# w_conv_out in two seven-product units behind three gate pairs, in the mixer of a two-layer encoder trunk

## The chip, the core and the metric

The kernel runs on one core of a Trainium2 chip. The metric is the device time of one launch in microseconds. Engines are named as the profile names them: PE (TensorE's matmuls), PEld (its weight loads), DVE (VectorE), ACT (ScalarE), POOL (GpSimd), SP (SyncE, which issues the weight loads here). L12 is line 12 of the kernel.

## The reference, cut to the mixer

640 tokens (512 of a prompt, 8 x 16 of running streams) of width 1024 pass two layers. Each layer is a half-step FFN, a mixer and a second half-step FFN. The change lies in the mixer, behind its convolution and attention:

```python
z = h @ w_in
cb, cc, cv, q, k, v, g = jnp.split(z, splits, axis=-1)
g = jax.nn.sigmoid(g + b_gate)                 # 2 x 1024 columns
g_conv, g_attn = jnp.split(g, 2, axis=-1)
y_conv, conv_new = _short_conv(cb, cc, cv, conv_prev, w_conv)    # 512 channels
y_attn, k_new, v_new = attn_fn(q, k, v)                          # 8 heads x 64
m = g_conv * (y_conv @ w_conv_out) + g_attn * (y_attn @ w_attn_out)
return m @ w_o, conv_new, k_new, v_new
```

w_conv_out and w_attn_out are 512 x 1024, w_o is 1024 x 1024. Everything is float32.

## The kernel before

**Numbers in two parts.** A float32 product is made of three matmuls of type fp32r: every operand is split into hi (a cast on ACT) and lo (the difference, on DVE), and hi x hi, hi x lo and lo x hi are added up in PSUM. Activations lie with channels in the 128 partitions and the 640 tokens in the free dimension; a matmul takes a 128 x 128 weight tile and half the tokens, 320 columns.

**By seven.** Where two rows of output tiles are made from pairs of input tiles, the kernel sees weights and inputs as 2 x 2 blocks (two output rows, two kinds of input tile, two halves of the tokens) and forms the four result blocks from seven products in place of eight (Strassen's way, in Winograd's form). The products are called X11, X21, XN6, XT5, XT7, X22 and XT4 after their input block; the inputs N6, T5, T7, T4 are sums and differences of input blocks, and the weights need four sums as well. The FFN's projections, the FFN's `down_rows`, and all columns of w_in but v run this way; w_conv_out, w_attn_out and w_o are plain products (`product`, L374 in the profile).

**Weights.** All weights come in one stream of 512 KB chunks of eight tiles in the order of use (`mixer_order`, `kinds`, `_stream`); SP loads them into three buffers. `source` makes the sums of a by-seven group (two chunks, called a, b here), `prep` the hi part, `flush` the lo part. A group gives four slabs: slab 0 is a, slab 1 is two sums of half a chunk, slab 2 is a with its second half replaced by a sum, slab 3 half of b. hi and lo parts lie in three buffers each, so slab i + 3 takes the buffer of slab i. `slab` moves on by one slab and prepares the one after the next; `quiet` moves on and prepares nothing; `ahead` makes the sums for the next slab not yet prepared; `begin` prepares one more slab.

**The stage.** `attention` ends with the gates of rows 0 and 1. Then `outputs` (layer 0: from 642 us, layer 1: from 1885 us) runs in an order that is written out: PE, DVE and ACT each take their instructions strictly as the code issues them. POOL and SP follow their own queues. The order of before is: gate pair 2 (rows 2 and 3 of the 16 gate rows); w_conv_out's rows 0 to 3; pair 4; rows 4, 5; pair 6; rows 6, 7; then for each of pairs 8 to 14 two rows of w_attn_out; then w_o.
- `gate_pair(m)`: the seven products in banks pa, pb, pc (four single PSUM banks go round). ACT copies the partial results that are used twice out of PSUM (L1281, L1291, L1293), DVE adds (L251), multiplies by the norm factor `rr` (L1297, L1303, L1306), ACT applies the sigmoid (L1129).
- `out(m, y)`: one plain product in a pair of banks (`acc`, two pairs go round), multiplied by its gate (L1323, L1325); for w_attn_out the result is added to the row of w_conv_out (`mm`).
- `take`: hi and lo parts of the convolution's output (in pair 2, behind X11) and of the attention's output (in pair 8, behind X11), four tiles of 640 columns each.

The convolution's output `ycs` lies in two tiles of two rows. In the attention they also serve as scratch for scores and for sums of inputs. `down_rows` in the FFN has the form that the new unit takes: two output rows of each kind in a pair of banks, and additions that POOL issues as an accumulating DMA (L984).

Of the kernel before, what the change touches and what calls it, by code (L numbers as in the profile page):

```python
# [22 lines left out]
T = SEQ + NB * TS  # L23
HT = T // 2
# [6 lines left out]
KT = D // P  # L31
FT = FF // P
FH = FT // 2
CT = CW // P
# [6 lines left out]
NP = KT // 2  # L41
# [16 lines left out]
XT4, XN6, XT7, X21, X22, X11, XT5 = range(7)  # L58
# [64 lines left out]


def kinds():


    out, inside = [], [False]

    def put(kind):  # L130
        out.append((kind, inside[0]))

    def plain(n):
        for kind in [8] * (n // 8) + [n % 8] * (n % 8 > 0):
# [24 lines left out]
    for l in range(L):  # L159
        ffn(f"a{l}")  # L160
        held = 0
        for what, _ in mixer_order():
            if what == "mix":
# [12 lines left out]


def halves(t):
    return t.rearrange("p (a b) -> p a b", a=2)
# [3 lines left out]
def trunk(ctx: ExitStack, tc: tile.TileContext, xin, wst, small, pbias, samplebias, kcache, vcache,  # L183
# [33 lines left out]
    def tmp(name):  # L217
        return tp.tile([P, UW], F32, tag="t", name=name)[:, :T]
# [31 lines left out]
    def add(out, a, b):  # L250
        DVE.tensor_tensor(out=out, in0=a, in1=b, op=ALU.add)  # L251
# [58 lines left out]
    def flush():  # L310
        for lo, src, hi in pending:
            DVE.tensor_tensor(out=lo, in0=src, in1=hi.bitcast(F32), op=ALU.subtract)  # L312
        pending.clear()
# [73 lines left out]
    def product(ps, ops, at=()):  # L387
        for _ in steps(ps, ops, at):
            pass

    def block(ps, s, half, ops, ks, start, stop):

        for kp in ks:
            w = [z[:, (half * NP + kp) * P : (half * NP + kp + 1) * P] for z in s]
            xh, xl = ops(kp)
            for j, (a, b) in enumerate(((w[0], xh), (w[0], xl), (w[1], xh))):
                PE.matmul(ps, a, b, start=start and kp == 0 and j == 0,  # L397
                          stop=stop and kp == NP - 1 and j == 2, skip_group_check=True)
# [713 lines left out]
    def mixer(l, after):  # L1112
        with tc.tile_pool(name=f"yp{l}", bufs=1, reuse_waits="tile") as yp, \
# [85 lines left out]
            with tc.tile_pool(name=f"gp{l}", bufs=1, reuse_waits="tile") as gp, \  # L1199
                 tc.manual_schedule(engines=ORDERED):  # L1200
                hold[0] = True
                mo = outputs(l, gp, ops.X, st, cs, ycs, yas, sigmoid, gates)
        ex = after()
        with tc.manual_schedule(engines=ORDERED):
            hold[0] = True
# [56 lines left out]
        def t5(self, kp):  # L1262
            self.parts(*(z[:, HT:] for z in self.h[2 * kp]), self.a[kp][:, 1])

    def outputs(l, gp, X, st, cs, ycs, yas, sigmoid, gates):


        rr, t1, t2 = st.rr, slice(0, HT), slice(HT, T)
        spare = [gp.tile([P, 2, T], F32, name=f"mm{l}_{i}") for i in range(2)]
        mm = ycs + [spare[i // 2][:, i % 2] for i in range(CT)]  # L1270
        X11, X21, X22, XN6, XT5, XT7, XT4 = (X[i] for i in ("11", "21", "22", "N6", "T5", "T7", "T4"))
        c1, u2, c5 = cs
        every = range(NP)

        def gate_pair(m, then=None):
            n = f"{l}_{m}"
            pa, pb, pc = (att(f"q{i}{n}")[:, :HT] for i in "abc")
            u, g = gates[m], gates[m + 1] = tmp(f"g{n}"), tmp(f"g{n}_1")
            s0 = quiet()
            block(pa, s0, 0, X11, every, True, True)  # L1280
            ACT.copy(c1, pa)  # L1281
            prep(used[0] + 1)
            flush()
            if then:
                then()
            block(pb, s0, 1, X21, every, True, True)
            add(u[:, t1], pb, c1)
            s1 = slab(True)[0]
            flush()
            block(pa, s1, 0, XN6, every, False, True)  # L1290
            ACT.copy(u2, pa)  # L1291
            block(pc, s1, 1, XT5, every, True, True)
            ACT.copy(c5, pc)  # L1293
            s2 = slab(True)[0]
            block(pa, s2, 0, XT7, every, False, True)
            add(g[:, t2], pa, c5)
            DVE.tensor_tensor(out=g[:, t2], in0=g[:, t2], in1=rr[:, t2], op=ALU.mult)  # L1297
            flush()
            ahead()
            block(pc, s2, 1, X22, every, False, True)  # L1300
            add(u[:, t2], pc, u2)
            s3 = slab(True)[0]
            DVE.tensor_tensor(out=u, in0=u, in1=rr, op=ALU.mult)  # L1303
            sigmoid(u, m)
            block(pa, s3, 0, XT4, every, False, True)
            DVE.tensor_tensor(out=g[:, t1], in0=pa, in1=rr[:, t1], op=ALU.mult)  # L1306
            sigmoid(g, m + 1, -1.0)
            flush()

        def parts(pool, tag, name, src):  # L1310
# [4 lines left out]
        def out(m, y, then=None):  # L1315

            py = acc(f"py{l}_{m}")
            product(py, y)
            if then:
                then()  # L1320
            g = gates[m]
            if m < KT:
                DVE.tensor_tensor(out=halves(mm[m]), in0=two(py), in1=halves(g), op=ALU.mult)  # L1323
            else:
                DVE.tensor_tensor(out=halves(g), in0=two(py), in1=halves(g), op=ALU.mult)  # L1325
                add(mm[m - KT], mm[m - KT], g)
            flush()

        yc, ya, mo = [], [], []

        def take(y, name, srcs):
            for c, src in enumerate(srcs):
                y.append(parts(gp, f"y{c}", f"{name}{l}_{c}", src))

        def give(ms):
            for m in ms:
                mo.append(parts(hp, "h", f"m{l}_{m}", mm[m]))

        gate_pair(2, lambda: take(yc, "yc", ycs))
        for m in range(4):  # L1340
            out(m, yc)
        for m in range(4, 2 * KT, 2):
            gate_pair(m, (lambda: take(ya, "ya", [yas[:, c, :] for c in range(CT)])) if m == KT else None)
            y = yc if m < KT else ya
            last = m == 2 * KT - 2
            out(m, y, (lambda: give(range(3))) if last else None)
            out(m + 1, y, (lambda: give(range(3, 6))) if last else None)
        give(range(6, KT))
        return mo

    def attention(l, h, norms, stats, ops, mp, yas, ycp, both, others):
# [423 lines left out]
def _stream(i):  # L1775
# [9 lines left out]
    for l in range(L):  # L1785
# [34 lines left out]
        for what, m in mixer_order():  # L1820
            if what == "v":
                out.append(v.reshape(KT // 2, 2, P, AW).transpose(0, 2, 1, 3).reshape(-1, P, CH))
            elif what == "mix":
                out.append(chunks(held))
                held = []

                out.append(chunks([rows[name][a][o::2] for name, a in m for o in range(2)]))
            else:
                held.append(rows[what][m])
        out.append(chunks(held))  # L1830
# [69 lines left out]
```

## Time and profile before

| | |
|---|---|
| median of three runs | 2514.66 us (2514.56 to 2515.52) |
| profiled execution, its own time | 2514.72 us |
| its span, first to last instruction | 2512.7 us |
| granted clock of TensorE | 0.999 |
| DMA, mean over the span | 109 GB/s |

The profile is of one execution. A row of a grouped view gives line, engine, operation, output and inputs, shape and count, then the busy time, the mean length in ns, and the idle time in front with what ended it. A timeline row gives the start and the length in us. A row of windows gives each engine's busy time and number of instructions in a stretch.

### The profile page before, as it was taken

What the parts mean: (1) busy time and instruction counts of PE and PEld (TensorE: products, weight loads), DVE (VectorE), ACT (ScalarE), POOL (GpSimd) and SP (SyncE); (2) the same over time, 40 slices, a digit from 0 to 9 for tenths busy, and PEclk for the clock granted to TensorE, in tenths of its full rate; (3) what the DMA queues carried; (4) which work ended last, traced back from release to release, by engine and by line L of the source; (5) the groups of instructions that cost most, each with busy time, mean ns of one, the idle gap of its engine ahead of it and who ended that gap; (6) DMA issues with size and microseconds to landing.
All of it is one profiled execution on the core that took longest, in us unless ns stands there. A gap on an engine that the chain in (4) does not pass through costs nothing.

```text
span 2512.7 us, 42964 instructions
## 1 busy us (share of the span) xinstructions
PE 2496.8 (99%) x17192; PEld 2440.6 (97%) x17192; DVE 2101.2 (84%) x3321; ACT 1342.7 (53%) x2112; POOL 216.3 (9%) x275
## 2 busy tenths in 40 slices
PE   9999999999999999999999999999999999999998
PEld 9999999888999999999999999998889999999998
DVE  7889888878677898988699889888786768889897
ACT  7445556665444545555455555556654455455553
POOL 0000112111000001110001011121110000010100
PEclk9999999999999999999999999999999999999999
DMA  4234554234222235443225453543342222254544
GB/s 145 76 103 116 126 126 127 107 114 162 76 85 93 76 102 126 111 121 105 85 76 118 121 127 106 126 118 125 128 139 85 76 93 76 85 121 119 127 113 99
DMA packets 106392, 273.92 MB, mean 109 GB/s; under 512 B 10096, under 2 KB 52208, under 8 KB 106192
## 3 DMA queue, kind: packets, MB, share of 16 engines
q1 hardware_dynamic: 69408, 220.76, 26.3%
q0 software_dynamic: 36064, 49.78, 11.6%
q8 instruction: 135, 2.21, 0.4%
q10 hardware_dynamic: 720, 0.65, 0.1%
q14 instruction: 65, 0.53, 0.1%
HBM read 222.70 MB, written 7.94 MB: 92 GB/s over the span
## 4 chain that ended last, share of the span: by engine, by line
PE 95%; DVE 3%; ACT 2%; issue 0%; DMA 0%; DVEq 0%; ACTq 0%
PE pab L397 12%; PE paa L397 11%; PE pcb L397 6%; PE pca L397 5%; PE daa L960 5%; PE py L374 4%; PE po L374 4%; PE qa L397 4%; PE dab L960 4%; PE pdb L374 4%; PE pbb L397 3%; PE pba L397 3%; PE dca L960 3%; PE poa L374 2%; PE pda L374 2%; PE pv L1404 2%
## 5 line engine op out<-in xcount | busy, mean ns | idle before, releaser
L312 DVE TENSOR_TENSOR wlo<-raw,whi 128x1024 fp32r<-128x1024 f32 (+1 forms) x566 | 585.4, 1037 | 189.3 <-ACT whi L307 184.7
L307 ACT CAST whi<-raw 128x1024 fp32r<-128x1024 f32 (+1 forms) x566 | 509.1, 903 | 369.2 <-PE pbb L397 38.4
L307 ACT CAST whi<-s 128x1024 fp32r<-128x1024 f32 (+1 forms) x152 | 144.4, 950 | 247.1 <-issue 89.4
L397 PE MATMUL pab<-xhib,whi 128*128 128x320 f32 x704 | 218.2, 310 | 0.0
L397 PE MATMUL pab<-xhib,wlo 128*128 128x320 f32 x704 | 217.7, 309 | 0.0
L397 PE MATMUL pab<-xlob,whi 128*128 128x320 f32 x704 | 217.5, 309 | 0.0
L397 PE MATMUL paa<-xhia,wlo 128*128 128x320 f32 x640 | 197.8, 309 | 0.7 <-DVE wlo L312 0.7
L397 PE MATMUL paa<-xhia,whi 128*128 128x320 f32 x640 | 197.9, 309 | 0.0
L397 PE MATMUL paa<-xloa,whi 128*128 128x320 f32 x640 | 197.6, 309 | 0.0
L312 DVE TENSOR_TENSOR wlo<-s,whi 128x1024 fp32r<-128x1024 f32 (+1 forms) x152 | 166.3, 1094 | 11.6 <-ACT whi L307 10.6
L984 POOL DMA_DIRECT2D x<-c_b x40 | 48.3, 1207 | 1083.8 <-ACT whi L307 475.6
L984 POOL DMA_DIRECT2D x<-c_a x50 | 60.6, 1214 | 837.4 <-ACT whi L307 402.8
L397 PEld LDWEIGHTS pab<-xhib,wlo 128*128 128x128 f32 x704 | 132.2, 188 | 0.3
L397 PEld LDWEIGHTS pab<-xhib,whi 128*128 128x128 f32 x704 | 132.2, 188 | 0.2
L397 PEld LDWEIGHTS pab<-xlob,whi 128*128 128x128 f32 x704 | 132.2, 188 | 0.2
L397 PEld LDWEIGHTS paa<-xhia,wlo 128*128 128x128 f32 x640 | 120.1, 188 | 1.3 <-DVE wlo L312 1.3
L397 PEld LDWEIGHTS paa<-xloa,whi 128*128 128x128 f32 x640 | 120.1, 188 | 0.1
L397 PEld LDWEIGHTS paa<-xhia,whi 128*128 128x128 f32 x640 | 120.1, 188 | 0.1
L397 PE MATMUL pcb<-xhib,wlo 128*128 128x320 f32 x352 | 109.0, 310 | 0.0
L397 PE MATMUL pcb<-xhib,whi 128*128 128x320 f32 x352 | 108.8, 309 | 0.0
L397 PE MATMUL pcb<-xlob,whi 128*128 128x320 f32 x352 | 108.7, 309 | 0.0
L251 DVE TENSOR_TENSOR raw<-raw,raw 128x512 f32<-128x512 f32 x152 | 103.8, 683 | 1.5 <-DMA raw<-in_wst 0.5
(682 smaller groups left out, 7927.1 us busy)
## 6 DMA issues: line engine op xcount, KB each, us to landing
raw<-in_wst SPq DMA_DIRECT2D x378, 512.0 KB, 3.5
x<-c_a POOLq DMA_DIRECT2D x50, 320.0 KB, 5.0
x<-c_b POOLq DMA_DIRECT2D x40, 320.0 KB, 4.5
kc<-in_kcache SPq DMA_DIRECT2D x32, 256.0 KB, 3.9
vc<-in_vcache SPq DMA_DIRECT2D x16, 512.0 KB, 4.6
x<-u_a POOLq DMA_DIRECT2D x18, 320.0 KB, 5.1
x<-u_b POOLq DMA_DIRECT2D x14, 320.0 KB, 4.8
bias<-in_pbias POOLq DMA_DIRECT2D x16, 256.0 KB, 3.3
```

The lines of the kernel that those rows point to most:

```text
L251: DVE.tensor_tensor(out=out, in0=a, in1=b, op=ALU.add)
L307: ACT.copy(hi[:, d], src[:, c])
L312: DVE.tensor_tensor(out=lo, in0=src, in1=hi.bitcast(F32), op=ALU.subtract)
L374: PE.matmul(ps[:, a, :HT], w, x[:, a * HT : (a + 1) * HT], start=first and j == 0, stop=last and j == 2)
L397: PE.matmul(ps, a, b, start=start and kp == 0 and j == 0, stop=stop and kp == NP - 1 and j == 2, skip_group_check=True)
L960: PE.matmul(ps[u], w, y, start=start and i == 0 and j == 0, stop=i == 1 and j == 2, skip_group_check=True)
L984: POOL.dma_start(rows(r, cols), z, accum_op=ALU.add)
L1404: PE.matmul(pv[t], xx[:, t * P : (t + 1) * P], w[:, kk * AW : (kk + 1) * AW], start=c == 0 and kk == 0 and j == 0, stop=c == KT // 2 - 1 a ...
```

## The change

w_conv_out is computed in two units of four output rows each (rows 0 to 3, rows 4 to 7), by seven. Each unit has two pairs of the output rows (r, r + 2) in one pair of banks, so a copy or addition takes both at once. The order becomes: gate pairs 2, 4, 6; unit 0; unit 4; pair 8 and so on as before. Small work is put at named places ("spots") of the pairs and units: `spot("g4", 3)` is in pair 4 behind the third slab's call, `spot("c0", 1)` in unit 0 in front of X21.

- Pairs 2, 4 and 6 (`direct` is false) no longer add on DVE: ACT copies the PSUM bank, and POOL issues a DMA that adds the copy to the gate row in SBUF. The factor `rr` (`scale`) and the sigmoid (`bend`) come one to two groups later.
- `opening`, `firsts`, `lasts`, `raw_low`, `sum_high`, `sum_low` make the seven input blocks of the convolution's output, in pairs 2, 4 and 6. Four tiles' rows lie in one tile `yc`.
- A unit's results go to `yc` (unit 0) and `spare` (unit 4); `weigh` multiplies them by the gates later, rows 0 to 3 in unit 4, rows 4 to 7 in pair 10.
- The attention output's parts use the memory of `xhi` and `xlo`; hi parts of tiles 0, 1 behind X11 of pair 8, their lo parts and the hi parts of tiles 2, 3 behind XN6, the last lo parts behind XT5.

```diff
-    out += gates[:2] + [("co", m) for m in range(4)]
-    for i, g in enumerate(gates[2:]):
-        name, m = ("co", 4 + 2 * i) if i < 2 else ("ao", 2 * i - 4)
-        out += [g, (name, m), (name, m + 1)]
+    out += gates[:4] + [("unit", ("co", 0)), ("unit", ("co", 4))]
+    for i, g in enumerate(gates[4:]):
+        out += [g, ("ao", 2 * i), ("ao", 2 * i + 1)]
...
-            ycp = [yp.tile([P, 2, T], F32, name=f"yc{l}_{c}") for c in range(CT // 2)]
-            ycs = [z[:, i] for z in ycp for i in range(2)]
+            yc = yp.tile([P, CT, T], F32, name=f"yc{l}")
+            ycp = [yc[:, 2 * i : 2 * i + 2] for i in range(CT // 2)]
+            ycs = [yc[:, i] for i in range(CT)]
...
+        def accumulate(out, z):
+            POOL.dma_start(out, z, accum_op=ALU.add)
...
+            def take(out, ps, c):
+                if direct:
+                    add(out, ps, out)
+                else:
+                    ACT.copy(c, ps)
+                    accumulate(out, c)
...
+            spot(me, 3)
+            if not direct:
+                take(u[:, t1], pb, cs[0])
+            block(pa, s2, 0, xT7, every, False, True)
+            take(g[:, t2], pa, cs[2])
             flush()
             ahead()
...
+        def scale(m):
+            def job():
+                times(gates[m], rr)
+                times(gates[m + 1][:, t2], rr[:, t2])
+            return job
+
+        def bend(m):
+            def job():
+                sigmoid(gates[m], m)
+                sigmoid(gates[m + 1], m + 1, -1.0)
+            return job
...
+        xhi, xlo = (gp.tile([P, 2, 7, HT], F32R, name=f"x{i}{l}") for i in ("hi", "lo"))
...
+        def opening():
+            high(slice(0, 2), 4, v[:, :, 0, 0])
+            for i in range(2):
+                high(i, slice(5, 7), v[:, i, 1])
+
+        def firsts():
+            low(slice(0, 2), 4, v[:, :, 0, 0])
+            DVE.tensor_tensor(out=v[:, :, 0, 0], in0=v[:, :, 0, 0], in1=v[:, :, 0, 1], op=ALU.subtract)
+
+        def lasts():
+            DVE.tensor_tensor(out=v[:, :, 0, 1], in0=v[:, :, 1, 1], in1=v[:, :, 0, 1], op=ALU.subtract)
+            for a, b in ((v[:, :, 0, 0], v[:, :, 1, 1]), (v[:, :, 1, 1], v[:, :, 1, 0])):
+                DVE.scalar_tensor_tensor(out=b, in0=a, scalar=-1.0, in1=b, op0=ALU.mult, op1=ALU.subtract)
...
+        def unit(m0, to):
...
+            A, B = (acc(f"{i}co{n}") for i in ("ba" if m0 else "ab"))
+            if m0:
+                A, B = B, A
+            C = [att(f"c{i}co{n}")[:, :HT] for i in range(2)]
...
+            s0 = quiet()
+            mul(a, s0, 0, X11, True)
+            copy(rows(0, t1))
+            prep(used[0] + 1)
+            begin()
+            flush()
+            spot(me, 1)
+            mul(b, s0, 1, X21, True)
+            add(rows(0, t1), two(B), rows(0, t1))
+            s1 = slab(True)[0]
+            flush()
+            mul(a, s1, 0, XN6, False)
+            copy(rows(0, t2))
+            spot(me, 2)
+            mul(C, s1, 1, XT5, True)
+            for i in range(2):
+                ACT.activation(rows(1, t2)[:, i], C[i], AF.Copy, scale=-1.0)
+            s2 = slab(True)[0]
+            spot(me, 3)
+            mul(a, s2, 0, XT7, False)
+            copy(z, -1.0)
+            flush()
+            ahead()
+            mul(C, s2, 1, X22, False)
+            for i in range(2):
+                add(rows(0, t2)[:, i], C[i], rows(0, t2)[:, i])
+            add(rows(1, t2), rows(1, t2), z)
+            s3 = slab(True)[0]
+            ahead()
+            mul(a, s3, 0, XT4, False)
+            copy(rows(1, t1), -1.0)
+            flush()
+            spot(me, 4)
...
+        at("g2", 1, opening)
+        at("g2", 2, firsts)
+        at("g2", 3, raw_low(0))
+        at("g2", 4, raw_low(1))
+        at("g4", 1, lasts)
+        at("g4", 3, sum_high(0))
+        at("g4", 4, sum_high(1))
+        at("g6", 1, sum_low(0))
+        at("g6", 2, sum_low(1))
+        at("g6", 3, scale(2))
+        at("g6", 4, bend(2))
+        at("c0", 1, scale(4))
+        at("c0", 2, bend(4))
+        at("c0", 3, scale(6))
+        at("c0", 4, bend(6))
+        at("c4", 2, weigh(0, 1))
+        at("c4", 4, weigh(2, 3))
+        at(f"g{KT}", 1, taken(0, 1))
+        at(f"g{KT}", 2, took(0, 1), taken(2, 3))
+        at(f"g{KT}", 3, took(2, 3))
+        at(f"g{KT + 2}", 2, weigh(5, 7))
+        at(f"g{KT + 2}", 4, weigh(4, 6))
+        for m in (2, 4, 6):
+            gate_pair(m)
+        unit(0, yc)
+        unit(CT, spare)
```

More of the change, by code (lines that the diff above doesn't have):

```diff
@@ L162, in kinds @@
         for what, _ in mixer_order():
-            if what == "mix":
+            if what in ("mix", "unit"):
                 plain(held)
@@ L1201, in mixer @@
                 hold[0] = True
-                mo = outputs(l, gp, ops.X, st, cs, ycs, yas, sigmoid, gates)
+                mo = outputs(l, gp, ops.X, st, cs, yc, yas, sigmoid, gates)
         ex = after()
@@ L1263, in t5, with outputs @@
             self.parts(*(z[:, HT:] for z in self.h[2 * kp]), self.a[kp][:, 1])
-    def outputs(l, gp, X, st, cs, ycs, yas, sigmoid, gates):
+    def outputs(l, gp, X, st, cs, yc, yas, sigmoid, gates):
         rr, t1, t2 = st.rr, slice(0, HT), slice(HT, T)
[L1269 to L1272, printed above, removed]
+        spare = gp.tile([P, CT, T], F32, name=f"mm{l}")
+        mm = [z[:, i] for z in (yc, spare) for i in range(CT)]
+        x11, x21, x22, xN6, xT5, xT7, xT4 = (X[i] for i in ("11", "21", "22", "N6", "T5", "T7", "T4"))
+        z = halves(st.caps)
@@ L1273, in outputs, with spot, at, times @@
         every = range(NP)
-        def gate_pair(m, then=None):
+        jobs = {}
+        def spot(at, i):
+            for job in jobs.pop((at, i), ()):
+                job()
+        def at(place, i, *fs):
+            jobs.setdefault((place, i), []).extend(fs)
+        def accumulate(out, z):
+            POOL.dma_start(out, z, accum_op=ALU.add)
+        def times(out, g):
+            DVE.tensor_tensor(out=out, in0=out, in1=g, op=ALU.mult)
+        def gate_pair(m):
             n = f"{l}_{m}"
@@ L1279, in gate_pair @@
             s0 = quiet()
-            block(pa, s0, 0, X11, every, True, True)
-            ACT.copy(c1, pa)
+            block(pa, s0, 0, x11, every, True, True)
+            ACT.copy(u[:, t1], pa)
             prep(used[0] + 1)
             flush()
[L1284 to L1287, printed above, removed]
+            spot(me, 1)
+            block(pb, s0, 1, x21, every, True, True)
+            if direct:
+                take(u[:, t1], pb, cs[0])
@@ L1288, in gate_pair @@
             s1 = slab(True)[0]
             flush()
[L1290 to L1293, printed above, removed]
-            s2 = slab(True)[0]
-            block(pa, s2, 0, XT7, every, False, True)
-            add(g[:, t2], pa, c5)
-            DVE.tensor_tensor(out=g[:, t2], in0=g[:, t2], in1=rr[:, t2], op=ALU.mult)
+            block(pa, s1, 0, xN6, every, False, True)
+            ACT.copy(u[:, t2], pa)
@@ L1298, in gate_pair @@
+            spot(me, 2)
+            block(pc, s1, 1, xT5, every, True, True)
+            ACT.copy(g[:, t2], pc)
+            s2 = slab(True)[0]
+            spot(me, 3)
+            if not direct:
+                take(u[:, t1], pb, cs[0])
+            block(pa, s2, 0, xT7, every, False, True)
+            take(g[:, t2], pa, cs[2])
             flush()
             ahead()
-            block(pc, s2, 1, X22, every, False, True)
-            add(u[:, t2], pc, u2)
+            block(pc, s2, 1, x22, every, False, True)
@@ L1302, in gate_pair @@
+            take(u[:, t2], pc, cs[1])
             s3 = slab(True)[0]
-            DVE.tensor_tensor(out=u, in0=u, in1=rr, op=ALU.mult)
-            sigmoid(u, m)
-            block(pa, s3, 0, XT4, every, False, True)
+            if direct:
+                times(g[:, t2], rr[:, t2])
+                times(u, rr)
+                sigmoid(u, m)
+            block(pa, s3, 0, xT4, every, False, True)
             DVE.tensor_tensor(out=g[:, t1], in0=pa, in1=rr[:, t1], op=ALU.mult)
-            sigmoid(g, m + 1, -1.0)
+            if direct:
+                sigmoid(g, m + 1, -1.0)
@@ new lines, in outputs, with high, low @@
+        pairs = [{k: (xhi[:, i, c], xlo[:, i, c]) for c, k in enumerate((XT5, XT7, XT4, XN6, X11, X21, X22))}
+                 for i in range(2)]
+        vs = [v[:, i].rearrange("p o t c -> p (o t) c") for i in range(2)]
+        def high(i, c, z):
+            ACT.copy(xhi[:, i, c], z)
+        def low(i, c, z):
+            DVE.tensor_tensor(out=xlo[:, i, c], in0=z, in1=xhi[:, i, c].bitcast(F32), op=ALU.subtract)
+        def opening():
+            high(slice(0, 2), 4, v[:, :, 0, 0])
+            for i in range(2):
+                high(i, slice(5, 7), v[:, i, 1])
@@ new lines, in raw_low, with sum_high, sum_low, mul @@
+        def raw_low(i):
+            return lambda: low(i, slice(5, 7), v[:, i, 1])
+        def sum_high(i):
+            return lambda: high(i, slice(0, 4), vs[i])
+        def sum_low(i):
+            return lambda: low(i, slice(0, 4), vs[i])
+        def unit(m0, to):
+            n = f"{l}_{m0}"
+            A, B = (acc(f"{i}co{n}") for i in ("ba" if m0 else "ab"))
+            if m0:
+                A, B = B, A
+            C = [att(f"c{i}co{n}")[:, :HT] for i in range(2)]
+            a, b = ([z[:, i, :HT] for i in range(2)] for z in (A, B))
+            me = f"c{m0}"
+            def mul(ps, s, half, kind, start):
+                for i in range(2):
+                    for k, pair in enumerate(pairs):
+                        kp = half * NP + 2 * i + k
+                        wh, wl = (z[:, kp * P : (kp + 1) * P] for z in s)
+                        xh, xl = pair[kind]
+                        for j, (w, y) in enumerate(((wh, xh), (wh, xl), (wl, xh))):
+                            PE.matmul(ps[i], w, y, start=start and k == 0 and j == 0,
+                                      stop=k == 1 and j == 2, skip_group_check=True)
+            def rows(r, c):
+                return to[:, r::2, c]
+            def copy(out, scale=1.0):
+                ACT.activation(out, two(A), AF.Copy, scale=scale)
+            s0 = quiet()
[4 more added lines that the diff above has]
+            flush()
+            spot(me, 1)
+            mul(b, s0, 1, X21, True)
[4 more added lines that the diff above has]
+            copy(rows(0, t2))
+            spot(me, 2)
+            mul(C, s1, 1, XT5, True)
[8 more added lines that the diff above has]
+            mul(C, s2, 1, X22, False)
+            for i in range(2):
+                add(rows(0, t2)[:, i], C[i], rows(0, t2)[:, i])
[5 more added lines that the diff above has]
+            flush()
+            spot(me, 4)
@@ L1310, in parts, with weigh, job @@
+        def weigh(*ms):
+            def job():
+                for m in ms:
+                    times(mm[m], gates[m])
+            return job
         def parts(pool, tag, name, src):
@@ L1313, in parts, with out @@
             return hi, lo
-        def out(m, y, then=None):
+        ya, mo = [], []
+        def out(m, then=None):
             py = acc(f"py{l}_{m}")
-            product(py, y)
+            product(py, ya)
             if then:
                 then()
[L1321 to L1326, printed above, removed]
+            g = gates[m + KT]
+            DVE.tensor_tensor(out=halves(g), in0=two(py), in1=halves(g), op=ALU.mult)
+            add(mm[m], mm[m], g)
             flush()
[L1329 to L1333, printed above, removed]
         def give(ms):
@@ L1337, in give, with taken, job, took @@
                 mo.append(parts(hp, "h", f"m{l}_{m}", mm[m]))
[L1339 to L1347, printed above, removed]
+        for c in range(CT):
+            ya.append(tuple(z[:, c // 2, :].rearrange("p a b -> p (a b)")[:, (c % 2) * T : (c % 2 + 1) * T]
+                            for z in (xhi, xlo)))
+        def taken(*cs):
+            def job():
+                for c in cs:
+                    ACT.copy(ya[c][0], yas[:, c, :])
+            return job
+        def took(*cs):
+            def job():
+                for c in cs:
+                    hi, lo = ya[c]
+                    DVE.tensor_tensor(out=lo, in0=yas[:, c, :], in1=hi.bitcast(F32), op=ALU.subtract)
+            return job
+        at("g2", 1, opening)
[24 more added lines that the diff above has]
+        unit(CT, spare)
+        for m in range(0, KT, 2):
+            gate_pair(m + KT)
+            last = m == KT - 2
+            out(m, (lambda: give(range(3))) if last else None)
+            out(m + 1, (lambda: give(range(3, 6))) if last else None)
         give(range(6, KT))
+        assert not jobs
         return mo
@@ L1827, in _stream @@
                 out.append(chunks([rows[name][a][o::2] for name, a in m for o in range(2)]))
+            elif what == "unit":
+                out.append(chunks(held))
+                held = []
+                name, a = m
+                out.append(chunks([rows[name][a + r + 2 * u][o::2] for r in range(2) for o in range(2)
+                                   for u in range(2)]))
             else:
```

9 lines of the change are left out of this document (8 added, 1 removed).

## The prediction

> **What bounds the kernel now.** I read the page first, for the engine that sets the end: the span, the busy times, and the engines of the chain that ended last.
>
> ```profile
> span 2512.7 us, 42964 instructions
> ...
> PE 2496.8 (99%) x17192; PEld 2440.6 (97%) x17192; DVE 2101.2 (84%) x3321; ACT 1342.7 (53%) x2112; POOL 216.3 (9%) x275
> ...
> PE 95%; DVE 3%; ACT 2%; issue 0%; DMA 0%; DVEq 0%; ACTq 0%
> ```
>
> TensorE is the chain. The next view is PE's waits over the whole span (us in total, times, longest).
>
> ```profile
> PE poa L374 <- ACT whi L620: 5.6, 1, 5.6
> ...
> PE paa L397 <- DVE wlo L312: 0.7, 2, 0.4
> ...
> PE po L374 <- DVE m_6lo L222: 0.4, 2, 0.2
> ```
>
> The largest wait is the kernel's start. Of the stage that is changed, only the end of the last output shows (m_6lo, 0.4 us in two layers), and the change leaves that alone. Then the stage in windows: layer 0's outputs begin at 642, layer 1's at 1885.
>
> ```profile
> core 0: us, PE busy (x) PEld busy (x) DVE busy (x) ACT busy (x) POOL busy (x), PEclk, DMA share, GB/s
> 642.00:700.00 58.00, 58.00 (x397) 57.99 (x396) 38.16 (x56) 24.91 (x37) 0.00 (x0) 1.00 0.25 82
> 660.00:720.00 60.00, 60.00 (x410) 60.00 (x409) 40.05 (x59) 23.50 (x36) 0.00 (x0) 1.00 0.23 73
> ...
> 1923.00:1983.00 60.00, 60.00 (x411) 60.00 (x410) 44.00 (x65) 26.09 (x39) 0.00 (x0) 1.00 0.25 82
> ```
>
> PE never rests there, and 410 matmuls take 60 us: **0.1463 us each**. That is the price of a matmul, not the mean that the groups show,
>
> ```profile
> L397 PE MATMUL paa<-xhia,whi 128*128 128x320 f32 x640 | 197.9, 309 | 0.0
> ```
>
> since two are in flight at a time. One product of 12 matmuls is 1.76 us, a gate pair or a unit (7 products) 12.3 us. VectorE is two thirds busy and GpSimd idle.
>
> **The matmuls.** w_conv_out falls from 8 outputs x 4 tiles x 3 x 2 halves = 192 matmuls to 2 units x 7 x 12 = 168 in a layer. Over two layers 48 go: 48 x 0.1463 = **7.0 us**, and nothing else can shorten a stage without PE waits. The Trainium skill (TensorE: Matmul & The Clock Gate, section "Back-to-back issue gap") gives N/2.4 + 2.5 ns for a lone warm matmul, which for 320 columns would be 136 ns and 6.5 us in all, as an estimate; the windows above measured 146 and decide.
>
> **What it costs the other engines.** Mean lengths by shape, from the grouped view of 640 to 800 us:
>
> ```profile
> L312 DVE TENSOR_TENSOR wlo<-raw,whi 128x1024 fp32r<-128x1024 f32 x24 | 29.3, 1219 | 10.0 <-ACT whi L307 10.0
> L312 DVE TENSOR_TENSOR wlo<-raw,whi 128x512 fp32r<-128x512 f32 x14 | 9.6, 682 | 0.0
> L1303 DVE TENSOR_TENSOR g<-g,rrm 128x640 f32<-128x640 f32 x7 | 5.8, 826 | 0.2
> L251 DVE TENSOR_TENSOR g<-qb,capsm 128x320 f32<-128x320 f32 x7 | 3.4, 483 | 0.0
> L1323 DVE TENSOR_TENSOR mm<-py,g 128x640 f32<-128x640 f32 x4 | 3.3, 821 | 2.9 <-PE py L374 2.9
> L307 ACT CAST whi<-raw 128x1024 fp32r<-128x1024 f32 x25 | 26.3, 1050 | 15.1 <-PE qc L397 14.0 <-DVE raw L251 0.6 <-ACT m_5hi L221 0.5
> L1129 ACT ACTIVATE g<-g,sm 128x640 f32<-128x640 f32 x16 | 12.5, 825 | 6.4 <-DVE g L1303 6.0 <-DVE g L1146 0.3
> ```
>
> The next instruction starts before the last one's row ends; the timeline shows by how much (start, length):
>
> ```profile
> 645.55 1.23 DVE L312 TENSOR_TENSOR wlo<-raw,whi 128x1024 fp32r<-128x1024 f32 x1 [1.26 <-ACT whi L307]
> 646.70 0.82 DVE L222 TENSOR_TENSOR yc_0lo<-yc,yc_0hi 128x640 fp32r<-128x640 f32 x1
> 647.43 0.82 DVE L222 TENSOR_TENSOR yc_1lo<-yc,yc_1hi 128x640 fp32r<-128x640 f32 x1
> ...
> 662.51 0.68 DVE L251 TENSOR_TENSOR raw<-raw,raw 128x512 f32<-128x512 f32 x1
> 663.22 0.69 DVE L251 TENSOR_TENSOR s<-raw,raw 128x512 f32<-128x512 f32 x1
> 663.83 0.68 DVE L251 TENSOR_TENSOR raw<-raw 128x512 f32<-128x512 f32 x1
> ```
>
> ```profile
> 644.15 0.43 ACT L1281 COPY capsm<-qa 128x320 f32<-128x320 f32 x1
> 644.47 1.05 ACT L307 CAST whi<-raw 128x1024 fp32r<-128x1024 f32 x1
> 645.42 0.73 ACT L221 CAST yc_0hi<-yc 128x640 fp32r<-128x640 f32 x1
> ...
> 647.93 0.62 ACT L307 CAST whi<-raw 128x512 fp32r<-128x512 f32 x1
> 648.45 0.42 ACT L1291 COPY capsm<-qa 128x320 f32<-128x320 f32 x1
> ...
> 654.72 1.55 ACT L1129 ACTIVATE g<-g,sm 128x640 f32<-128x640 f32 x2 [0.85 <-DVE g L1303]
> ```
>
> So VectorE is taken for 0.60 us by 512 columns, 0.73 by 640, 1.13 by 1024, and 0.73 by 512 whose result the next one reads (662.51 to 663.22). The row less 0.09 gives 0.40 for 320; reading PSUM costs the same (821 against 826). ScalarE: 0.32, 0.53 (647.93 to 648.45), 0.63, 0.95, and 0.73 a sigmoid (1.55 for two). 1280 columns, which the change brings, I extend from 512 and 1024: 1.40 and 1.16. ScalarE's copy of two PSUM banks has a row in the FFN:
>
> ```profile
> L974 ACT ACTIVATE c_a<-daa x32: 688/706/712, 170.9 to 1648.2; 128x640 f32<-128x640 f32 x32
> ```
>
> Weights by seven cost VectorE two lo parts of 1024, three of 512 and four sums of 512: 6.5 us in each pair and each unit. A pair that sends its additions to GpSimd adds 0.4, and later 1.13 for its two scales: 8.0. A unit adds 0.73 + 2 x 0.4 + 0.73: 8.7. The operands: three lo parts and four differences of 640, 5.1, and two lo parts of 1280, 2.8; in all 7.9. `weigh(0..3)` is 2.9. Together 3 x 8.0 + 2 x 8.7 + 7.9 + 2.9 = **52.2 us of VectorE against 61.5 us of PE** (5 x 12.3). It fits, at 85%, but each pair and unit must deliver its weights in turn, and the order on ScalarE and VectorE is strict, so I walked it.
>
> **The walk.** Weight slabs lie in three buffers, so a slab is made two ahead. As a test, the same durations in the order of before, from the first matmul of pair 2 at 642.19, put that of pair 4 at 668.56 where the trace has
>
> ```profile
> 668.61 0.31 PE L397 MATMUL qa<-hhim,whi 128*128 128x320 f32 x1
> ```
>
> In the new order pairs 2, 4 and 6 leave PE without a wait. What is late afterwards is one chain ScalarE - VectorE - ScalarE. Times count from the first matmul of unit 0; pair 6 began at -12.3.
> - Pair 6, VectorE: lo of slab 2 at -8.6, `sum_low(0)` -7.5, lo of slab 3 -6.1, `sum_low(1)` -5.5, `scale(2)` -4.1 to -2.9, lo of unit 0's slab 0, then three sums of slab 1, the last ending at 0.3.
> - ScalarE: slab 1's second cast 0.4 to 0.9, `bend(2)` (two sigmoids) to 2.35, copy of X11 to 2.97, cast of slab 2, its end 4.0. Slab 3's cast, put here by `begin`, needs the buffer of slab 0, free when X21 ends at 3.5: no wait, and behind it only the copy after XN6, at 5.3.
> - VectorE: lo of slab 2 from 4.06 and slab 3 to 5.8, `scale(4)`'s first half ends 6.6.
> - ScalarE: `bend(4)` waited for it, 6.65 to 8.1; the two copies of C to 8.76 (X22, due at 8.8, needs the first then and the second 0.9 later); cast of unit 4's slab 0 ends 9.8.
> - VectorE: its lo from 9.85, the three sums end at 13.1.
> - ScalarE: second cast of slab 1 at 13.15, and only then unit 0's last copy, 13.7 to 14.4.
> **First wait:** unit 4's X21 (due at 8 x 1.76 = 14.06) writes the banks that this copy empties: 0.4 us. Behind the copy stands `bend(6)`, 1.46 us, then unit 4's first copy, 15.76 to 16.5. **Second wait:** unit 4's XN6 adds to the bank this copy reads, due at 14.44 + 1.76 = 16.2: 0.3 us. In unit 4 `weigh` has room (no `scale`, no `bend`), and pair 8 finds its slabs made. So 0.7 us in a layer, **1.4 us** in two.
>
> Bounds of it: 0 if ScalarE runs a little ahead; above, every one of the dozen hand-overs above 0.1 us longer (dependent sums show such a gap, 0.73 for 0.60), 1.9 us a layer, 3.8 in two. I take 1.4.
>
> Edits that cost nothing: `take` for conv and its eight PSUM multiplications leave VectorE, which had room, so PE gains nothing. The attention output's parts are hidden by pair 8's 12.3 us, before and after, and the windows show no wait there to win back; without that cover they would cost their 4 x 0.73. Weight bytes stay, but pairs that follow each other free their buffers later: a pair's second chunk takes the buffer that slab 2's lo part leaves some 4.8 us into the pair before,
>
> ```profile
> raw<-in_wst SPq DMA_DIRECT2D x378, 512.0 KB, 3.5
> ```
>
> lands at 8.3 and is summed from 10.5 on, so 2 us are to spare; each us beyond would delay the chain by as much. The eighteen added GpSimd additions (nine a layer, 160 KB) go through an idle engine; the FFN shows their price and landing:
>
> ```profile
> L984 POOL DMA_DIRECT2D x<-c_a x50: 1192/1202/1389, 177.8 to 1657.2; - x50
> ...
> DMA to landing us min/median/max: 4.1/4.9/8.3
> ```
>
> POOL has nothing else queued in this stage. Pair 2's additions have over 15 us until `scale(2)`, pair 4's as much until `scale(4)`. Pair 6's last is issued at -0.5 and `scale(6)` reads it at 7.7: covered up to 8.2 us.
>
> **Sum:** 2514.72 (profiled execution: span 2512.7 and 2.0 around it) - 7.0 + 1.4 = **2509.1 us**; the median before lies 0.06 lower, which I neglect.
>
> **The rivals.**
> - *No wait at all:* all seven products hidden, 2514.7 - 7.0 = 2507.7. For it: the two waits are 0.3 to 0.4 us, of the size of what the walk leaves out. Against: both come from one strict queue. Chance 0.21.
> - *The chain turns slower:* both units at the upper bound, 2514.7 - 7.0 + 3.8 = 2511.5. For it: dependent instructions dominate there. Chance 0.13.
> - *VectorE is held while GpSimd issues an addition* (slower). Nine issues of 1.2 us are 10.8 us a layer. If they stop VectorE, at most the 61.5 - 52.2 = 9.3 us that it has free can take them, and since most of that is waiting in the chain, I put half of it: 10.8 - 4.6 = 6.2 us a layer, 2509.1 + 12.4 = 2521.5. It loses from 2.8 us a layer on. Against it stand VectorE's rows during two such issues, at their usual lengths:
>
> ```profile
> 177.75 2.63 POOL L984 DMA_DIRECT2D x<-c_a  x2 [172.98 <-ACT c_a L977]
> ...
> 178.46 0.69 DVE L251 TENSOR_TENSOR raw<-raw,raw 128x512 f32<-128x512 f32 x1
> 179.47 0.68 DVE L251 TENSOR_TENSOR raw<-s,raw 128x512 f32<-128x512 f32 x1
> ```
>
> The Trainium skill (SBUF — State Buffer, section "Who interferes with whom") has VectorE's instructions with two SBUF inputs contend with a GpSimd instruction that reads SBUF; by that rule this rival would hold if issuing an addition reads SBUF, and these rows, 0.69 and 0.68 against a mean of 0.68, do not bear it out. Chance 0.07.
> - *Additions land late:* VectorE's `scale(6)` waits, and all weights behind it. Slower than before from a landing of about 11 us on (8.2 + 2.8), against 8.3 as the largest in that row; at 12 us, 2 x 3.8 us more: 2516.7. Chance 0.04.
>
> **How the numbers follow.** A measurement of this kernel tells about 0.2% (5.0 us) from no change: the line is at 2509.6. My own case (chance 0.55, 2508.0 to 2510.8) lies close to it; I give three quarters of it to faster, 0.41, since its waits are single ones and small. With the first rival: faster 0.62; same 0.14 + 0.13 = 0.27; slower 0.11. The range, 2507.3 to 2513.0, holds the first three cases, with 0.4 us below for runs and 1.5 above the upper bound for hand-overs that no row shows.
>
> **What would show it.** 48 matmuls fewer and 1.76 us a product in the units; PE waits on ScalarE's copies in unit 4's X21 and XN6, 0.2 to 0.6 us each, and none in pairs 2, 4, 6; GpSimd's eighteen issues of 1.2 us with VectorE's 512-column rows still at 0.68. Wrong would be: PE waiting for wlo in pairs 4 or 6 (VectorE behind, not ScalarE), VectorE's scales waiting for DMA, or a longer attention stage, where the joined tile is scratch.

## The result, and the profile after

| | before | changed |
|---|---|---|
| median (11 runs each) | 2515.45 us (2514.56 to 2516.06) | 2509.33 us (2508.33 to 2510.05) |
| profiled execution, its own time | 2514.72 us | 2508.88 us |
| its span | 2512.7 us | 2507.1 us |

The ratio is 0.9976, with a 95% interval from 0.9967 to 0.9984: 0.24% faster, close to the 0.2% that the prediction drew as the line. The changed kernel is 0.2 us above the predicted time by the median and 0.2 below it by the profiled execution. The prediction forecast 5.6 us less, from one profiled execution of before that lies 0.7 us under this median of before; the medians differ by 6.1 us, the profiled executions by 5.84. So the fair measure of its sum is 5.6 against 5.84, and the closeness of the median to 2509.1 is in part luck.

The page of the changed kernel, its span, busy times and the engines of the chain that ended last:

```profile
span 2507.1 us, 43020 instructions
...
PE 2491.1 (99%) x17144; PEld 2433.9 (97%) x17144; DVE 2127.9 (85%) x3357; ACT 1371.6 (55%) x2168; POOL 231.8 (9%) x293
...
PE 94%; DVE 3%; ACT 2%; issue 0%; DMA 0%; DVEq 0%; ACTq 0%
```

48 matmuls fewer (17192 to 17144), 36 VectorE instructions, 56 ScalarE instructions and 18 GpSimd instructions more. TensorE is still the chain.

The stage by windows, columns as before (us and instructions of PE, PEld, DVE, ACT, POOL, then granted clock, DMA share, GB/s):

```profile
642.00:702.00 60.00, 59.95 (x407) 59.41 (x406) 50.05 (x69) 40.51 (x66) 7.81 (x9) 1.00 0.42 113
660.00:720.00 60.00, 59.95 (x407) 59.42 (x406) 54.23 (x78) 39.61 (x62) 5.19 (x6) 1.00 0.40 113
1883.00:1943.00 60.00, 59.94 (x407) 59.41 (x406) 50.01 (x69) 40.03 (x65) 7.84 (x9) 1.00 0.42 113
```

PE's own column barely moves: a wait here is about as long as the row of the matmul still in flight (0.3 us), so hardly any of it shows as idle time. The count moves: 407 in place of 410 or 411. Three matmuls or so, about 0.5 us, are missing in each layer. The waits of PE's weight loads show them (us in total, times, longest), from 640 to 735:

```profile
PEld bco L1409 <- ACT yc L1416: 0.3, 1, 0.3
PEld aco L1409 <- ACT mm L1416: 0.3, 1, 0.3
```

bco is the bank pair that unit 4's X21 writes, aco the one that its XN6 adds to; L1416 is ScalarE's copy of a bank pair. Layer 1 shows the same two waits. The starts on PE give the size of both:

```profile
693.13 0.30 PE L1409 MATMUL aco<-xhi,wlo 128*128 128x320 f32 x1
693.48 0.42 PE L1409 MATMUL bco<-xhi,whi 128*128 128x320 f32 x1
693.74 0.31 PE L1409 MATMUL bco<-xlo,whi 128*128 128x320 f32 x1
...
695.20 0.31 PE L1409 MATMUL bco<-xhi,wlo 128*128 128x320 f32 x1
695.51 0.42 PE L1409 MATMUL aco<-xhi,whi 128*128 128x320 f32 x1
695.77 0.30 PE L1409 MATMUL aco<-xlo,whi 128*128 128x320 f32 x1
```

The row behind a wait opens early and is longer (0.42 for 0.31), so I read over two steps of 0.146 us: 693.74 - 693.13 - 2 x 0.146 = 0.32 us and 695.77 - 695.20 - 2 x 0.146 = 0.28 us. Together 0.6 us a layer.

For the experiments one length is enough: S, from the first matmul of pair 2 to the first of pair 10 in layer 0 (pair 2's start is taken one step of 0.146 before its second row). The two ends, in the timeline of before and of after:

```profile
642.34 0.31 PE L397 MATMUL qa<-hlom,whi 128*128 128x320 f32 x1
...
726.75 0.31 PE L397 MATMUL qa<-hhim,whi 128*128 128x320 f32 x1
```

```profile
642.30 0.31 PE L396 MATMUL qa<-hlom,whi 128*128 128x320 f32 x1
...
723.80 0.31 PE L396 MATMUL qa<-hhim,whi 128*128 128x320 f32 x1
```

S is 726.75 - 642.19 = 84.56 before and 723.80 - 642.16 = 81.64 after (from starts with three digits; the rows as shown give 642.15 and 81.65); layer 1 gives 84.56 and 81.65. Of the 24 matmuls' 3.52 us, 2.92 arrived: 0.6 went into the two waits.

The whole difference of the profiled executions, 5.84 us, closes: 2 x 2.92 = 5.84 come from the stage, and two small differences cancel. The time around the span is 0.2 shorter (1.8 against 2.0), and the wait at the kernel's start is 0.2 longer than the 5.6 of before:

```profile
PE poa L373 <- ACT whi L619: 5.8, 1, 5.8
```

### The profile page after: what moved, and what is told of

Same layout as the page of the kernel before. It is cut to its first block, busy times and chain, and to the rows that moved or that the text cites. A ratio compares the mean times of both kernels' runs of the same rounds, so it can differ in the third digit from the quotient of the medians.

```text
span 2507.1 us, 43020 instructions
## 1 busy us (share of the span) xinstructions
PE 2491.1 (99%) x17144; PEld 2433.9 (97%) x17144; DVE 2127.9 (85%) x3357; ACT 1371.6 (55%) x2168; POOL 231.8 (9%) x293
## 4 chain that ended last, share of the span: by engine, by line
PE 94%; DVE 3%; ACT 2%; issue 0%; DMA 0%; DVEq 0%; ACTq 0%
PE pab L396 12%; PE paa L396 11%; PE pcb L396 6%; PE pca L396 5%; PE daa L959 5%; PE po L373 4%; PE dab L959 4%; PE qa L396 4%; PE pdb L373 4%; PE pbb L396 3%; PE pba L396 3%; PE dca L959 3%; PE poa L373 2%; PE pda L373 2%; PE pv L1585 2%; PE ma_cv L396 2%
```

## The experiments

**1. Where each wait comes from.** Three kernels. The first puts `bend(6)` behind unit 4's first copy.

```diff
-        at("c0", 4, bend(6))
+        at("c4", 1, bend(6))
```

> The sigmoids of pair 6, bend(6), stand in unit 4 in front of X21 instead of at the end of unit 0. Measure: the stretch from the first matmul of pair 2 to the first matmul of pair 10 in layer 0, 84.56 us before and 81.65 us in the changed kernel, which 24 matmuls less at 0.1465 us alone would make 81.04. Theory (each of the two PE waits has its own queue in front of it on ScalarE): the wait in unit 4's XN6 goes, the one in its X21 stays, stretch 81.35, about 0.6 us less in two layers. Rival (one late chain: what is taken away in one place comes back in the next product): stretch stays at 81.65.

S was 724.12 - 642.75 = 81.37, the time 2508.37 us (one run). Of the two waits only one is left:

```profile
PEld bco L1409 <- ACT yc L1416: 0.3, 1, 0.3
```

So XN6's wait was `bend(6)`, 0.27 us, and X21's does not depend on it. The second puts a unit's last copy ahead of the casts of the next slab 1.

```diff
-            s3 = slab(True)[0]
-            ahead()
+            flush()
+            s3 = quiet()
             mul(a, s3, 0, XT4, False)
             copy(rows(1, t1), -1.0)
+            prep(used[0] + 1)
+            ahead()
             flush()
```

> In both units the last copy out of PSUM stands on ScalarE in front of the casts of the next slab, not behind them. Theory: the wait in unit 4's X21 goes, but the casts and bend(6) now end 0.6 us later against PE, so the wait in XN6 grows from 0.28 to about 0.6; stretch 81.5. If the two waits were independent: XN6 stays at 0.28, stretch 81.3.

S was 723.99 - 642.36 = 81.63, the time 2508.74 us (one run): no gain at all. The wait of X21 is gone and that of XN6 has doubled, in the waits of PE's weight loads:

```profile
PEld aco L1409 <- ACT mm L1416: 0.6, 1, 0.6
```

ScalarE's timeline in this kernel tells why. Unit 0 begins at 679.39 here.

```profile
691.91 0.71 ACT L1416 ACTIVATE yc<-aco 128x640 f32<-128x640 f32 x1 [2.23 <-PE aco L1409]
692.51 0.62 ACT L306 CAST whi<-s 128x512 fp32r<-128x512 f32 x1
693.02 0.62 ACT L306 CAST whi<-raw 128x512 fp32r<-128x512 f32 x1
693.54 0.83 ACT L1129 ACTIVATE g_6a<-g_6a,sm 128x640 f32<-128x640 f32 x1
694.27 0.82 ACT L1129 ACTIVATE g_6b<-g_6b,sm 128x640 f32<-128x640 f32 x1
694.99 0.69 ACT L1416 ACTIVATE mm<-aco 128x640 f32<-128x640 f32 x1
```

The first copy now ends 13.2 us into the unit, before X21 is due. But the same five instructions stand ahead of unit 4's first copy, so that one still ends at 695.68, 16.3 into the unit, where it ended in the changed kernel. PE comes to XN6 earlier by what it no longer waits at X21 and loses it there. I had expected a part of that; it was all. The third kernel makes both edits.

> Both edits together. Theory: no PE wait is left in the units, the stretch is 81.05, which is the count of matmuls alone, and the kernel takes 1.2 us less than the changed one, about 2508.1 us in the median, 0.9972 of before. Rival (the chain between ScalarE and VectorE is late by itself): a wait of 0.3 us or more shows up elsewhere in unit 4 or pair 8, stretch 81.4 or more.

S was 723.66 - 642.62 = 81.04 in both layers, which is 84.56 - 3.52: no loss left. PE's count in the window is that of before:

```profile
642.00:702.00 60.00, 60.00 (x411) 59.98 (x410) 50.60 (x71) 40.87 (x67) 7.81 (x9) 1.00 0.44 112
```

The time is 2507.83 us (2507.47 to 2508.36, six runs), ratio to before 0.9969 (0.9957 to 0.9981). It is the fastest version found that makes all the products. Against the changed kernel the medians differ by 1.5 us and the profiled spans by 0.9, where S says 1.2; the runs were made on different occasions, and the intervals of the two ratios overlap, so it is the trace that separates them.

**2. The order and the small pieces alone.** The new order, GpSimd's additions and the late lo parts stay, but w_conv_out is eight plain products again, with the scales and sigmoids between them.

```diff
-    out += gates[:4] + [("unit", ("co", 0)), ("unit", ("co", 4))]
+    out += gates[:4] + [("co", m) for m in range(KT)]
...
-        unit(0, yc)
-        unit(CT, spare)
+        for m in range(KT):
+            row(m)
```

> The order and the GpSimd additions of the changed kernel, with w_conv_out as eight plain products behind pairs 2, 4 and 6. Theory (the gain is the count of matmuls and nothing else): 192 matmuls a layer again, stretch 84.5 us, time as before within 1 us. Rival (part of the gain is from the order or from work taken off VectorE): stretch below 84.2 and time 1 us or more under before. A stretch above 84.8 would mean that three pairs back to back cost waits of their own.

S was 727.07 - 642.51 = 84.56, before's own figure; the time 2515.47 us (2515.16 to 2516.07), ratio 1.0 (0.9991 to 1.0009). Nine GpSimd additions run in the window and PE does not notice:

```profile
642.00:702.00 60.00, 60.00 (x411) 59.99 (x411) 36.97 (x50) 30.19 (x48) 7.79 (x9) 1.00 0.43 113
```

The attention's parts by themselves, in the kernel before:

```diff
...
-            gate_pair(m, (lambda: take(ya, "ya", [yas[:, c, :] for c in range(CT)])) if m == KT else None)
+            gate_pair(m, *((lambda: taken(0, 1), lambda: (took(0, 1), taken(2, 3)), lambda: took(2, 3)) if m == KT else ()))
...
```

> The kernel before, with only the attention output's hi and lo parts spread over three places of pair 8. Theory: hidden before and after, stretch 84.56 and time as before. Rival (it was part of the gain): stretch shorter by 0.2 us or more.

S 84.56 again, 2515.23 us (one run) beside a median before of 2515.30. The whole gain lies in the units' matmuls.

**3. How near the edge the chain of ScalarE and VectorE is.** Here VectorE does the additions, scales and sigmoid order of pairs 2, 4 and 6 itself, as before the change, while the units and the blocks' parts stay.

```diff
-            direct = m >= KT
+            direct = True
...
-        at("g6", 3, scale(2))
-        at("g6", 4, bend(2))
-        at("c0", 1, scale(4))
-        at("c0", 2, bend(4))
-        at("c0", 3, scale(6))
-        at("c0", 4, bend(6))
```

> Pairs 2, 4 and 6 add on VectorE at once as pairs 8 to 14 do, with their scales and sigmoids inside the pair; GpSimd issues nothing in this stage. VectorE's sum over pairs 2 to unit 4 rises by 3 x 3 x 0.4 = 3.6 us to 55.8 of 61.5. Theory (strict order, one chain of ScalarE and VectorE): about 4 us of PE waits a layer in X21 of pairs 4 and 6 (for a bank that VectorE empties late) and XN6 of pair 6 and unit 0; stretch 85.0, the whole gain of the seven products lost, time 2515 to 2517. Rival (what counts is VectorE's sum against PE's): it still fits, stretch 81.7, time as the changed kernel.

S was 728.83 - 642.28 = 86.55 and the time 2518.86 us (2517.63 to 2520.61, ten runs), ratio 1.0013 (1.0004 to 1.0023): 0.13% slower than before, and the stretch 1.5 us a layer longer than the 85.0 expected. PE's weight loads wait:

```profile
PEld qa L396 <- ACT g_6a L1309: 2.5, 1, 2.5
PEld aco L1409 <- ACT yc L1416: 0.8, 1, 0.8
PEld qa L396 <- ACT g_4a L1309: 0.5, 1, 0.5
PEld qa L396 <- DVE g_4b L250: 0.3, 1, 0.3
```

That is 4.1 us, where about 4 was expected. The two largest are ones that were named: XN6 of pair 6 (behind the copy L1309 of g_6a) and of unit 0 (aco). X21 of pairs 4 and 6, named as well, do not wait; in their place pair 4's XN6 (g_4a) and XT4 (g_4b) do. So the size came out better than the places. The other 1.4 us (86.55 - 81.04 - 4.1) is not a wait. The same kernel in windows around the longest of them:

```profile
671.00:673.60 2.60, 0.38 (x3) 0.11 (x2) 1.70 (x3) 2.60 (x5) 0.00 (x0) 1.00 0.00 0
673.60:674.60 1.00, 1.00 (x6) 1.00 (x7) 0.07 (x1) 1.00 (x2) 0.00 (x0) 0.93 0.00 0
674.60:677.80 3.20, 3.20 (x14) 3.20 (x13) 3.20 (x4) 0.84 (x2) 0.00 (x0) 0.50 0.32 87
677.80:680.00 2.20, 2.20 (x17) 2.20 (x16) 1.76 (x2) 1.04 (x2) 0.00 (x0) 0.98 0.65 197
```

After the gap TensorE was granted half its clock for the whole third window, and for a little of its neighbours: 0.93 over 1.0 us and 0.98 over 2.2 us are another 0.2 us at half. That makes about 3.4 us. Its timeline:

```profile
671.07 0.31 PE L396 MATMUL qb<-hhim,wlo 128*128 128x320 f32 x1
673.60 0.41 PE L396 MATMUL qa<-thi,whi 128*128 128x320 f32 x1 [2.22 <-ACT g_6a L1309]
...
674.94 0.47 PE L396 MATMUL qa<-tlo,whi 128*128 128x320 f32 x1
675.21 0.47 PE L396 MATMUL qa<-thi,wlo 128*128 128x320 f32 x1
```

Starts are 0.267 us apart in place of 0.146: 3.4 / 0.267 = 13 matmuls, each 0.12 late, about 1.5 us, which is the missing 1.4 within the rounding of the waits. So a wait of 2.5 us cost about 4.0.

The other direction: the units' matmuls lose a third, while the work of ScalarE and VectorE stays. If PE bound the units, S would fall by 56 x 0.146 = 8.2 us.

```diff
-                        for j, (w, y) in enumerate(((wh, xh), (wh, xl), (wl, xh))):
+                        for j, (w, y) in enumerate(((wh, xh), (wh, xl))):
                             PE.matmul(ps[i], w, y, start=start and k == 0 and j == 0,
-                                      stop=k == 1 and j == 2, skip_group_check=True)
+                                      stop=k == 1 and j == 1, skip_group_check=True)
```

> The changed kernel with the products of the weights' lo parts left out of the two units: 8 matmuls a product, 56 fewer a layer, 8.2 us of PE. All work of the other engines stays. Theory (the chain of ScalarE and VectorE is right behind PE): PE waits in the units take nearly all of it, stretch 81.0 to 81.5, time within 1.5 us of the changed kernel. Rival (PE is the bound with room beneath): stretch 73.4, time 16.4 us less.

S was 723.07 - 642.32 = 80.75, 0.9 us less than in the changed kernel; the time 2507.43 us (2506.78 to 2507.98, six runs), ratio 0.9967 (0.9955 to 0.998). Of 16.4 us in two layers 1.9 came. The bound that I had set, 81.0, was a little too high. The units in windows:

```profile
678.00:702.00 24.00, 19.44 (x126) 18.14 (x125) 20.55 (x31) 17.58 (x28) 0.92 (x2) 1.00 0.37 106
```

PE rests for 4.6 of 24 us and VectorE is at 86%. The waits of PE's weight loads add up to 8.0 us in eight places: five copies of ScalarE in the units, and three in pair 8, two of them behind VectorE. So nearly all of the 8.2 us that PE saved has turned into waits for the chain. In this order of instructions the chain has 0.3 us a layer to give beyond 81.04, the length without waits; no run tried it with the order of the third kernel of experiment 1. It is the second limit, close behind PE.

**4. VectorE beside GpSimd's issuing.** Each addition is cut in two, 36 issues in place of 18.

```diff
-            POOL.dma_start(out, z, accum_op=ALU.add)
+            for c in (slice(0, HT // 2), slice(HT // 2, HT)):
+                POOL.dma_start(out[:, c], z[:, c], accum_op=ALU.add)
```

> Each of GpSimd's additions in pairs 2, 4 and 6 is issued as two of half the columns: 36 issues in place of 18. Theory (an issue does not hold VectorE): VectorE's 512-column rows during issues stay at 0.68 to 0.69 us, the stretch at 81.65, the time as the changed kernel. Rival (VectorE is held while GpSimd issues): rows beside an issue get longer by up to its length, stretch above 82.5.

S was 724.85 - 643.20 = 81.65, as with 18 issues; the time 2509.82 us (one run). GpSimd's timeline and VectorE's beside it, in this kernel:

```profile
652.45 1.77 POOL L1285 DMA_DIRECT2D g<-capsm  x2 [37.93 <-ACT capsm L1305]
653.58 2.39 POOL L1285 DMA_DIRECT2D g<-c  x2
```

```profile
653.16 0.69 DVE L250 TENSOR_TENSOR raw<-raw,raw 128x512 f32<-128x512 f32 x1
653.88 0.69 DVE L250 TENSOR_TENSOR s<-raw,raw 128x512 f32<-128x512 f32 x1
654.50 0.68 DVE L250 TENSOR_TENSOR raw<-raw 128x512 f32<-128x512 f32 x1
```

Sums with two SBUF inputs take their usual length through all of it.

## Why the prediction was right

**The bound and the count.** PE sets the stage, and removed matmuls are worth their step. S without waits is shorter by 3.52 us a layer, 24 x 0.1465, as the no-wait kernel shows to the hundredth. The term of 7.0 us stands.

**The two waits.** They are the ones named, in unit 4's X21 and XN6, and no other pair or unit waits: 0.32 and 0.28 us, where the walk had 0.4 and 0.3, 1.2 us in all where it had 1.4. ScalarE's timeline after, to be held against the walk's times from unit 0's first matmul (679.20 here), follows:

```profile
692.21 0.62 ACT L306 CAST whi<-raw 128x512 fp32r<-128x512 f32 x1
692.73 0.70 ACT L1416 ACTIVATE yc<-aco 128x640 f32<-128x640 f32 x1
693.33 0.82 ACT L1129 ACTIVATE g_6a<-g_6a,sm 128x640 f32<-128x640 f32 x1
694.04 0.82 ACT L1129 ACTIVATE g_6b<-g_6b,sm 128x640 f32<-128x640 f32 x1
694.77 0.69 ACT L1416 ACTIVATE mm<-aco 128x640 f32<-128x640 f32 x1
```

Unit 0's last copy ran from 13.53 to 14.23 (walk: 13.7 to 14.4), unit 4's first from 15.57 to 16.26 (15.76 to 16.5). The walk was 0.2 us late after the dozen hand-overs. It also let PE start at the very end of a copy, where PE's step began 0.17 us behind it (693.28 due + 0.32 = 693.60 against 693.43). The two small errors have opposite signs, which helped the size. Experiment 1 shows the causes apart: `bend(6)` for the one, the casts ahead of the copy for the other.

**One queue.** The prediction worked out the second wait behind the first (due at 14.44 + 1.76), so adding the two was right. What it did not say is that to remove the first alone gains nothing. Its own numbers hold that too: without the first wait XN6 is due at 14.06 + 1.76 = 15.82, and the copy still ends at 16.5, 0.7 us later. Experiment 1 measured 0.6 in one wait.

**Lengths that no row showed.** 1280 columns on VectorE and ScalarE, start to start, in the timelines after:

```profile
671.65 1.49 DVE L1367 TENSOR_TENSOR xlo<-yc,xhi 128x1280 fp32r<-128x1280 f32 x1
673.06 0.68 DVE L311 TENSOR_TENSOR wlo<-raw,whi 128x512 fp32r<-128x512 f32 x1
```

```profile
663.01 1.27 ACT L1364 CAST xhi<-yc 128x1280 fp32r<-128x1280 f32 x1
664.17 0.43 ACT L1304 COPY capsm<-qb 128x320 f32<-128x320 f32 x1
```

1.41 and 1.16, where 1.40 and 1.16 were extended from 512 and 1024.

**The edits at nothing** cost nothing: the order, the additions and the lo parts together and the lo parts alone left S at 84.56. The attention stage, where the joined tile is scratch, did not get longer: pair 2 begins at 642.16 against 642.19. GpSimd's additions land sooner than the FFN's, which are twice as large, and well within the 8 us that the tightest of them had by the walk; no run issued them later, so how near they are to hurting is not shown:

```profile
DMA to landing us min/median/max: 2.8/3.4/4.6
```

**The rivals.** *No wait at all* fell by the two waits; with two small moves it becomes true, 2507.83 measured for its 2507.7. *The chain turns slower* did not happen: the hand-overs that it put 0.1 us longer came out a little shorter. But the chain is as near the edge as it feared: with the old additions and the old places of scales and sigmoids it costs 5.5 us a layer (86.55 against 81.04: 4.1 of waits and 1.4 of half clock), and with a third of the units' matmuls gone the stretch falls by only 0.9. *VectorE is held* fell: twice the issues, the same S, rows of 0.68 and 0.69. (A layer's nine issues also took 7.8 us in the windows, where this rival counted 10.8.) By the rule that the prediction cited for it (the Trainium skill, SBUF — State Buffer, section "Who interferes with whom"), issuing an addition does not count here as an instruction that reads SBUF. *Additions land late* needed 11 us and the longest took 4.6.

**What stayed uncertain** was whether the gain is clear of 0.2%: 2509.1 was put at the line of 2509.6, and the interval of the ratio, 0.16% to 0.33%, reaches to both sides of 0.2% as well.

Both expectations of experiment 3 missed their size: one by 1.5 us above 85.0, for the clock, which the walk did not have, and one by 0.25 below the range's lower end of 81.0.

## What to carry to other kernels

Where TensorE never rested, a removed matmul was worth exactly its start-to-start step (0.1465 us here), and the question was only which strict queue becomes late next. A walk of those queues with start-to-start times found both waits in their places, with their sizes to 0.1 us. Two short waits behind one queue are one wait: moving unit 0's last copy ahead of the casts only moved the wait to the next copy, and it went when the sigmoids too were put behind that next copy. Before more matmuls are taken out of such a stage, take VectorE and ScalarE work out of it: with 56 fewer in a layer S fell by 0.9 us.

## What the runs showed of the hardware

A single wait of 2.5 us (experiment 3) was followed by about 3.4 us at a granted clock of 0.50. The half clock began about 1 us after PE had work again, not in the gap, and it raised the wait's price by more than half. Layer 1 shows it again: a wait of 2.6 us, and about 3.4 us of half clock from 1.5 us after it. In the kernel with a third of the units' matmuls removed the granted clock stayed at 1.00, with waits of up to 1.9 us:

```profile
PEld c0co L1409 <- ACT yc L1434: 1.9, 1, 1.9
PEld bco L1409 <- ACT yc L1416: 1.6, 1, 1.6
```

So a wait of 1.9 us left the clock whole and one of 2.5 us did not; no run tried a length between, or the same length at other moments, so it is not shown that the length alone decides. The Trainium skill (TensorE: Matmul & The Clock Gate, section "What's actually happening") puts the half clock behind at least one idle window of about 3.4 us, of windows that run on freely. The 3.4 us of half clock fit one such window; the gap of 2.5 us is shorter than that rule asks for, and the measurement decides.
